# A hybrid decoder block on one Trainium2 core: scaling the last output tiles on ScalarE and POOL, and taking the root of x's normalisation in PSUM

## The chip, the core and the metric

The kernel runs on one core of one Trainium2 chip. The metric is the time of one execution in device microseconds. The kernel before was timed three times: 2665.58, 2668.71 and 2671.58 us, median 2668.71 us.

The engines are named as the profile names them: PE is TensorE (PEld its weight loads), DVE is VectorE, ACT is ScalarE, POOL is GpSimd, SP issues all the DMAs that this text speaks of. SBUF is the on-chip working memory, PSUM the eight banks into which PE writes.

## The reference, cut to what matters

One layer of a decoder block on 2048 tokens of 1024 channels. A normalised and modulated input goes through one wide projection; two branches (a causal convolution and an RWKV-7 state recurrence) work on its parts, are projected, merged and projected once more; the result is added to x and normalised by a root mean square.

```python
h = _rmsnorm(x, norm_g) * (1.0 + scale) + shift           # x's normalisation
p = h @ w_in                                              # 1024 x 9344
y_conv = _conv_branch(...); y_rwkv = _rwkv7_branch(...)   # each ends in a 1024 x 1024 product
m = sigmoid(g_conv) * y_conv + sigmoid(g_rwkv) * y_rwkv
x = x + gate * (m @ w_out)
return _rmsnorm(x, final_g)                               # y * rsqrt(mean(y*y) + eps) * final_g

def _rmsnorm(x, g):
    y = x * lax.rsqrt(jnp.mean(x * x, axis=-1, keepdims=True) + RMS_EPS)
    return y * g
```

## The kernel before, in words

**Stages.** The tokens go in four blocks of 512. For each block the wide projection runs as 73 tiles of 128 output channels, each summed over eight pieces of the 1024 input channels; each fp32 product is made as three products of halves (`h_hi,w_hi`, `h_lo,w_hi`, `h_hi,w_lo`), so 24 matmuls of 128x512 a tile, written to `ps_main`. Beside it the convolution runs on DVE (`acc<-u,ck,acc`), and the recurrence runs in groups of heads as a chain of small matmuls (`aux`, `late`, `xo`) with DVE, ACT and POOL between them. A stage of output products follows: the RWKV branch's, the convolution branch's and the last one (`ro`, `co`, `o`), for blocks 0 and 1 and then for blocks 2 and 3, each as seven products of quarter matrices whose weights are called `w_c`. The last of them, `o` on blocks 2 and 3, ends the program.

**x's normalisation** (`xnorm`, L736). It is made for block b+1 while block b is worked on: ACT squares the tiles of x and leaves row sums in the small tile `st` (the profile calls it `ss`; 128 partitions by five rows of four numbers). When all are there, DVE adds the two halves of the sums (L758), divides and adds epsilon (L759), and takes the reciprocal root by `rsteps` (L380): a first guess from the bits and three Newton rounds of three instructions, ten small instructions of 128x4, with a wait for DVE's queue before every third. All operands are in SBUF. PE then turns the four columns into rows (`late<-ident,ss`, into the only PSUM bank tagged `late`), ACT copies them, and two DMAs spread them over the partitions. That happens three times in the program, for blocks 1, 2 and 3. The bank `late` is also used by the recurrence's chains and by other norms. For the last block's convolution norm the kernel has a second form of the root, `proot` (L392), that already runs with its variance and its running product in PSUM.

**The end** (`final`, L2210, inner function `finish`, L2252 to L2280). The last product leaves 16 tiles of 128x512 (two blocks `b_`, four groups of 128 tokens `n`, two halves `h_`). For each, DVE adds x to the PSUM result, ACT squares it and leaves the row sum in `sqm` (block 3) or `sqn` (block 2). For each pair of halves DVE takes the root as eight 128x1 instructions (the profile's `v<-sqm` or `v<-sqn` and seven `v<-v`), then scales both tiles by root and `final_g` in one instruction each (`scalar_tensor_tensor`, `cells<-cells,v,fg` or `fc<-fc,v,fg`), and SP sends each tile out.

**What sets the order.** Nothing in the program runs by itself: it is written as tasks (Python generators) that yield conditions, and a model of the engines' times (`note`, L118) decides which task goes on next: `ok(t)` waits until a tile is ready by the model, `idle("DVE", ...)` until DVE's queue is nearly empty, `bank("late")` until that PSUM bank is free, `burst` adds a lag for PE. The same model picks POOL or DVE for some subtractions (`w_lo`, `w_c`, `h_lo`). So an edit to one task moves the instructions of the others, for the rest of the program.

Of the kernel before, what the change touches and what calls it, by code (L numbers as in the profile page):

```python
# [13 lines left out]
ALU = mybir.AluOpType  # L14
# [4 lines left out]
P = 128  # L19
D = 1024  # L20
KT = D // P
TB = 512
NTT = TB // P
# [36 lines left out]
AHEAD = 0.7  # L60
# [24 lines left out]
def hybrid_block(ctx: ExitStack, tc: tile.TileContext, x, x_t, vecs, convk, w2a2, final_g, ada, w_in, w_co, w_ro, w_o, crow, out,  # L85
# [127 lines left out]
    nc = Lanes()  # L213
# [41 lines left out]
    def ok(*aps):  # L255
        ks = [key(a) for a in aps]
        return lambda: max(ready[q] for q in ks)
# [5 lines left out]
    def idle(name, us):  # L263
        return lambda: vt[name] - us
# [24 lines left out]
    def burst(*ws):  # L289
        w = both(*ws)  # L290

        def f():
            r = w()
            if r is None:
                return r
            return r + lag[0]

        return f
# [437 lines left out]
    def xnorm(b, tts):  # L736
        if not tts:
            return
        if tts[0] == 0:
            sums_[b] = e2.tile([P, 5, NTT], F32, name="ss0", tag="ss0", bufs=1)  # L740
        st = sums_[b]
        for tt in tts:
            t0 = b * TB + tt * P
            xh = []
            yield hx.room(2, 1)
            for half in range(2):
                xt = hx.take("xt")
                nc.sync.dma_start(xt, x[t0:t0 + P, half * TB:half * TB + TB])
                xh.append(xt)
            for half in range(2):  # L750
                yield ok(xh[half])
                nc.scalar.activation(xh[half], xh[half], AF.Square, accum_out=st[:, half, tt:tt + 1])
                hx.give(xh[half])
        if tts[-1] + 1 < NTT:
            return
        vs, rs, t_ = st[:, 2, :], st[:, 3, :], st[:, 4, :]
        yield both(ok(st), idle("DVE", AHEAD + 0.1))
        nc.vector.tensor_tensor(out=vs, in0=st[:, 0, :], in1=st[:, 1, :], op=ALU.add)  # L758
        nc.vector.tensor_scalar(out=vs, in0=vs, scalar1=1.0 / D, scalar2=RMS_EPS, op0=ALU.mult, op1=ALU.add)  # L759
        for n, _ in enumerate(rsteps(rs, vs, t_)):  # L760
            if n % 3 == 0:
                yield idle("DVE", AHEAD + 0.1)
        yield burst(ok(st), free, bank("late"), hx.room(2, 1))
        pt = pl.tile([P, TB], F32, name="late", tag="late")
        nc.tensor.transpose(pt[0:NTT, 0:P], rs, ident)
        gt, row = hx.take("gt"), hx.take("xrow")
        nc.scalar.copy(gt[0:NTT, 0:P], pt[0:NTT, 0:P])
        yield ok(gt)
        nc.sync.dma_start(xrow_d[b].rearrange("(n p) -> n p", p=P), gt[0:NTT, 0:P])
        hx.give(gt)  # L770
        nc.sync.dma_start(row, xrow_d[b].unsqueeze(0).broadcast_to([P, TB]))
        nxt = []

        def xload(k):
            nxt.append(hx.take("xf"))
            nc.sync.dma_start(nxt[-1], x_t[k, :, b * TB:b * TB + TB])

        yield hx.room(1, 1)
        xload(0)
        for k in range(KT):  # L780
            if k + 1 < KT:
                yield hx.room(1, 1)
                xload(k + 1)
            xf = nxt.pop(0)
            yield ok(xf, row)
            nc.gpsimd.tensor_tensor(out=xf, in0=xf, in1=row, op=ALU.mult)
            yield ok(xf)
            nc.scalar.activation(xf, xf, AF.Identity, scale=g_col[:, k:k + 1], bias=shift_col[:, k:k + 1])
            yield ok(xf)
            nc.sync.dma_start(xT_dram[b][k], xf)  # L790
            hx.give(xf)
        hx.give(row)
# [975 lines left out]
    with tc.manual_schedule():  # L1768
# [441 lines left out]
        def final(b0):  # L2210
            until(lambda: "sp" in more_)
            last = b0 + 2 == NB
            order_ = [(h_, b_, n) for h_, b_ in ((0, 0), (1, 1), (0, 1), (1, 0)) for n in range(4)]
            feed = Feed(fc, [x[(b0 + b_) * TB + n * P:(b0 + b_) * TB + n * P + P, h_ * TB:h_ * TB + TB]
                             for h_, b_, n in order_])
            have = {}
            sp, fg = more_["sp"], more_["fg"]
            if last:
                sq = [[sp.tile([P, 1, 2], F32, name="sqn", tag="sqn", bufs=4) for _ in range(4)]]
                s2 = [sp.tile([P, 2, 2], F32, name="sqm", tag="sqm", bufs=2) for _ in range(2)]  # L2220
                sq.append([s2[n // 2][:, n % 2:n % 2 + 1, :] for n in range(4)])
            else:
                s8 = sp.tile([P, 2, 4, 2], F32, name="sq8", tag="sq8", bufs=1)
                sq = [[s8[:, b_, n:n + 1, :] for n in range(4)] for b_ in range(2)]

            def plus(h_, b_, n, t_, ps):
                f = order_.index((h_, b_, n))
                yield feed.has(f)
                xt = feed.got[f]
                yield ok(xt)  # L2230
                nc.vector.tensor_tensor(out=t_, in0=ps, in1=xt, op=ALU.add)
                fc.give(xt)

            class Done:

                def __call__(self, h_, b_, n, t_):
                    Task(self.square(h_, b_, n, t_, oc), 1)

                def psum(self, n, ps):
                    f = order_.index((1, 0, n))  # L2240
                    yield feed.has(f)
                    xt = feed.got[f]
                    yield from padd(xt, ps, xt)
                    Task(self.square(1, 0, n, xt, fc), 1)

                def square(self, h_, b_, n, t_, home):
                    yield ok(t_)
                    fsq = sp.tile([P, TB], F32, name="fsq", tag="fsq", bufs=1)
                    nc.scalar.activation(fsq, t_, AF.Square, accum_out=sq[b_][n][:, 0, h_:h_ + 1])
                    have[b_, n, h_] = t_, home  # L2250

            def finish(b_, ns):  # L2252
                m = len(ns)
                yield when(lambda: all((b_, n, h_) in have for n in ns for h_ in range(2)))
                v3 = sp.tile([P, 3, 4], F32, name="v3", tag="v3", bufs=2)
                vs, rs, rt = [v3[:, i_, :m] for i_ in range(3)]
                yield both(ok(sq[b_][ns[0]]), idle("DVE", AHEAD))
                s_ = s8[:, b_] if m > 1 else sq[b_][ns[0]]
                if m > 1:
                    nc.vector.tensor_tensor(out=vs, in0=s_[:, :, 0], in1=s_[:, :, 1], op=ALU.add)  # L2260
                    nc.vector.tensor_scalar(out=vs, in0=vs, scalar1=1.0 / D, scalar2=RMS_EPS, op0=ALU.mult, op1=ALU.add)
                    rsqrt(rs, vs, None, nc.vector, rt)
                    nc.vector.tensor_scalar(out=rs, in0=rs, scalar1=-256.0, scalar2=None, op0=ALU.mult)
                else:
                    nc.vector.tensor_scalar(out=vs, in0=s_[:, :, 0], scalar1=s_[:, 0, 1:2], scalar2=D * RMS_EPS, op0=ALU.add,
                                            op1=ALU.add)
                    nc.vector.tensor_scalar(out=rs.bitcast(I32), in0=vs.bitcast(I32), scalar1=-0.5, scalar2=float(0x5F3759DF),
                                            op0=ALU.mult, op1=ALU.add)
                    for z_ in (3.0, 12.0, 768.0):
                        nc.vector.tensor_scalar(out=rt, in0=rs, scalar1=rs, scalar2=vs, op0=ALU.mult, op1=ALU.mult)  # L2270
                        nc.vector.tensor_scalar(out=rs, in0=rt, scalar1=z_, scalar2=rs, op0=ALU.subtract, op1=ALU.mult)
                for i, n in enumerate(ns):
                    t0 = (b0 + b_) * TB + n * P
                    for h_ in range(2):
                        t_, home = have[b_, n, h_]
                        yield both(ok(t_, rs), idle("DVE", AHEAD))
                        nc.vector.scalar_tensor_tensor(out=t_, in0=t_, scalar=rs[:, i:i + 1],
                                                       in1=fg[:, h_ * TB:h_ * TB + TB], op0=ALU.mult, op1=ALU.mult)
                        nc.sync.dma_start(out[t0:t0 + P, h_ * TB:h_ * TB + TB], t_)
                        home.give(t_)  # L2280

            for b_ in (1, 0):
                for ns in ([[0], [1], [2], [3]] if last else [[0, 1, 2, 3]]):
                    Task(finish(b_, ns), 2)
            return sums8(held(), held(), held(), Done(), plus)
# [51 lines left out]
```

## Time and profile before

| what | us |
|---|---|
| median of three runs | 2668.71 |
| the profiled execution's own time | 2668.12 |
| its span, from the first to the last instruction | 2666.4 |
| PE busy | 2588.4 |
| DVE busy | 2145.6 |
| POOL busy | 1343.5 |
| ACT busy | 1193.7 |
| PE idle while it waited for x's root (once) | 2.9 |
| from PE's last matmul to the span's end | 16.7 |

All instructions carry one line number, L196, since a helper records them; they are told apart by the names of their tiles, written out<-in. In a timeline a row is a start, a duration, an engine and an instruction; `x7` are seven in a row that belong together, and the brackets give idle time of the engine before it with what ended that. In a table by windows a row gives the stretch, then the busy time of PE, PEld, DVE, ACT and POOL with their counts, the clock that was granted to PE (1.00 is full), and DMA.

### The profile page before, as it was taken

To read this page: it belongs to the slowest core of one execution; us is meant where nothing else is said; L and a number is where in the kernel's file an instruction comes from. 1 tells how busy PE (TensorE), PEld (TensorE's weight loads), DVE (VectorE), ACT (ScalarE), POOL (GpSimd) and SP (SyncE) were. 2 spreads that over 40 slices of the span, in tenths; PEclk is the share of its full clock that TensorE was granted. 3 is DMA by queue.
4 is the path that set the end of the run, shared out by engine and by line. 5 is a ranking of instruction groups with operands and counts; after the bars stand their busy time and mean duration, and the time that the engine had idled before them with its cause. 6 is when DMAs were issued, how large, how long until landed. Compare 5 with 4: busy or idle time off the path is not lost. (4 is left out here: it accounts for less than half of the span.)

```text
span 2666.4 us, 50801 instructions
## 1 busy us (share of the span) xinstructions
PE 2588.4 (97%) x18335; PEld 2081.0 (78%) x18335; DVE 2145.6 (80%) x3631; ACT 1193.7 (45%) x2316; POOL 1343.5 (50%) x1842
## 2 busy tenths in 40 slices
PE   8999999999999999999999999999999998899997
PEld 6777887878878877888778887788887777678886
DVE  6786879798879786987687868888988678988687
ACT  6444444443344433443444343434444454456443
POOL 3575849462648374716483756483727586000000
PEclk9999999999999999999999999999999999999998
DMA  9888787887777778858786888786766787799984
GB/s 375 285 307 305 253 270 265 269 287 242 267 246 268 241 254 279 294 183 280 256 282 217 290 276 267 235 309 217 263 201 208 228 309 251 275 336 323 330 272 155
DMA packets 390559, 711.34 MB, mean 267 GB/s; under 512 B 137482, under 2 KB 141922, under 8 KB 390307
## 3 DMA queue, kind: packets, MB, share of 16 engines
q1 hardware_dynamic: 390306, 708.09, 78.7%
q8 instruction: 145, 2.38, 0.4%
q14 instruction: 108, 0.88, 0.1%
HBM read 493.82 MB, written 213.00 MB: 265 GB/s over the span
## 5 line engine op out<-in xcount | busy, mean ns | idle before, releaser
L196 PE MATMUL ps_main<-h_hi,w_lo 128*128 128x512 f32 x2304 | 923.9, 401 | 5.2 <-POOL w_lo L196 4.7
L196 PE MATMUL ps_main<-h_hi,w_hi 128*128 128x512 f32 x2304 | 923.2, 401 | 4.9 <-DVE vv L196 2.7
L196 PE MATMUL ps_main<-h_lo,w_hi 128*128 128x512 f32 x2304 | 921.5, 400 | 0.0
L196 DVE SCALAR_TENSOR_TENSOR acc<-u,ck,acc 128x512 f32<-128x512 f32 x928 | 698.4, 753 | 26.4
L196 PEld LDWEIGHTS ps_main<-h_hi,w_lo 128*128 128x128 f32 x2304 | 434.3, 188 | 102.4 <-POOL w_lo L196 6.4
L196 PEld LDWEIGHTS ps_main<-h_hi,w_hi 128*128 128x128 f32 x2304 | 434.3, 188 | 102.4 <-issue 6.7
L196 PEld LDWEIGHTS ps_main<-h_lo,w_hi 128*128 128x128 f32 x2304 | 434.2, 188 | 91.7 <-issue 4.5
L196 PE MATMUL ps_main<-h_hi,w_c 128*128 128x512 f32 x896 | 289.2, 401 | 6.7 <-POOL w_c L196 4.5
L196 ACT ACTIVATE th<-ps_main 128x512 f32<-128x512 f32 x160 | 95.7, 598 | 289.3 <-PE ps_main L196 276.5
L196 POOL TENSOR_TENSOR itmp<-La,TT 128x126 f32<-128x126 f32 (+22 forms) x496 | 199.5, 402 | 49.8 <-issue 16.4
L196 POOL TENSOR_TENSOR TT<-TT,itmp 128x126 f32<-128x126 f32 (+22 forms) x496 | 204.3, 412 | 38.9
L196 PEld LDWEIGHTS ps_main<-h_hi,w_c 128*128 128x128 f32 x896 | 170.5, 191 | 50.4 <-POOL w_c L196 6.7
L196 POOL TENSOR_TENSOR w_lo<-w_st,w_hi 128x1024 fp32r<-128x1024 f32 x60 | 145.3, 2422 | 106.6 <-ACT w_hi L196 87.0
L196 PE MATMUL ps_main<-h_lo,w_c 128*128 128x512 f32 x448 | 180.0, 402 | 7.2 <-DVE h_lo L196 7.2
L196 ACT COPY uv<-xo 64x256 f32<-64x256 f32 (+1 forms) x192 | 81.1, 439 | 196.4 <-PE xo L196 138.0
L196 DVE SCALAR_TENSOR_TENSOR S<-xo,pe,Se 64x64 f32<-64x64 f32 x512 | 123.1, 280 | 48.3 <-PE xo L196 38.5
L196 PE MATMUL ps_main<-w_c,h_hi 128*128 128x512 f32 x448 | 140.3, 393 | 0.0
L196 ACT CAST w_c<-w_raw 128x512 fp32r<-128x512 f32 x168 | 102.2, 618 | 71.8 <-DMA w_raw<-wk_o 23.0
L196 DVE TENSOR_TENSOR As<-aux,maskA 128x512 f32<-128x512 f32 x128 | 82.4, 686 | 49.9 <-PE aux L196 49.3
L196 ACT ACTIVATE Se<-S,pe 128x128 f32<-128x128 f32 x256 | 88.6, 394 | 44.5 <-DVE S L196 43.5
L196 PEld LDWEIGHTS ps_main<-h_lo,w_c 128*128 128x128 f32 x448 | 85.7, 191 | 27.5 <-DVE h_lo L196 8.5
L196 ACT ACTIVATE t<-ps_main,mu 128x512 f32<-128x512 f32 x96 | 65.9, 687 | 86.6 <-PE ps_main L196 86.1
(305 smaller groups left out, 4507.1 us busy)
## 6 DMA issues: line engine op xcount, KB each, us to landing
w_hi<-kh_in SPq DMA_DIRECT2D x219, 512.0 KB
w_lo<-kl_in SPq DMA_DIRECT2D x219, 512.0 KB
w_st<-w_in_t SPq DMA_DIRECT2D x73, 512.0 KB
kh_in<-w_hi SPq DMA_DIRECT2D x70, 512.0 KB
kl_in<-w_lo SPq DMA_DIRECT2D x70, 512.0 KB
lny<-y_d SPq DMA_DIRECT2D x80, 256.0 KB
w_raw<-wk_o SPq DMA_DIRECT2D x56, 256.0 KB
ada_st<-ada_t SPq DMA_DIRECT2D x16, 512.0 KB
```

Of the source, the lines that this page charges most:

```text
L196: r = f(*a, **k)
```

## The change

Two edits.

1. **`xnorm`.** The sum of the two halves still goes to `st` in SBUF, but the bank `late` is taken right then, ahead of the root instead of after it. The variance `vs` and Newton's running product are columns of that bank, and the root is taken by `proot`, without waits between its instructions. Only the result `rs` is in SBUF. The transpose goes into columns of the same bank, after a wait for the result and for PE.
2. **`finish`, in the last product.** For all of block 3 and for the first two token groups of block 2, 12 of the 16 tiles, DVE's scaling is replaced by two instructions: ACT multiplies the tile by the root (`nc.scalar.mul`), POOL multiplies it by `final_g`. The last four tiles (groups 2 and 3 of block 2) stay on DVE.

```diff
-        vs, rs, t_ = st[:, 2, :], st[:, 3, :], st[:, 4, :]
+        rs, sm = st[:, 3, :], st[:, 2, :]
         yield both(ok(st), idle("DVE", AHEAD + 0.1))
-        nc.vector.tensor_tensor(out=vs, in0=st[:, 0, :], in1=st[:, 1, :], op=ALU.add)
-        nc.vector.tensor_scalar(out=vs, in0=vs, scalar1=1.0 / D, scalar2=RMS_EPS, op0=ALU.mult, op1=ALU.add)
-        for n, _ in enumerate(rsteps(rs, vs, t_)):
-            if n % 3 == 0:
-                yield idle("DVE", AHEAD + 0.1)
-        yield burst(ok(st), free, bank("late"), hx.room(2, 1))
+        nc.vector.tensor_tensor(out=sm, in0=st[:, 0, :], in1=st[:, 1, :], op=ALU.add)
+        yield both(idle("DVE", AHEAD + 0.1), bank("late"), hx.room(2, 1))
         pt = pl.tile([P, TB], F32, name="late", tag="late")
+        vs = pt[:, P:P + NTT]
+        nc.vector.tensor_scalar(out=vs, in0=sm, scalar1=1.0 / D, scalar2=RMS_EPS, op0=ALU.mult, op1=ALU.add)
+        proot(rs, vs, pt[:, 2 * P:2 * P + NTT])
+        yield burst(ok(st), free)
         nc.tensor.transpose(pt[0:NTT, 0:P], rs, ident)
...
-                        yield both(ok(t_, rs), idle("DVE", AHEAD))
-                        nc.vector.scalar_tensor_tensor(out=t_, in0=t_, scalar=rs[:, i:i + 1],
-                                                       in1=fg[:, h_ * TB:h_ * TB + TB], op0=ALU.mult, op1=ALU.mult)
+                        if last and (b_ or n < 2):
+                            yield ok(t_, rs)
+                            nc.scalar.mul(t_, t_, rs[:, i:i + 1])
+                            yield ok(t_)
+                            nc.gpsimd.tensor_tensor(out=t_, in0=t_, in1=fg[:, h_ * TB:h_ * TB + TB], op=ALU.mult)
+                        else:
+                            yield both(ok(t_, rs), idle("DVE", AHEAD))
+                            nc.vector.scalar_tensor_tensor(out=t_, in0=t_, scalar=rs[:, i:i + 1],
+                                                           in1=fg[:, h_ * TB:h_ * TB + TB], op0=ALU.mult, op1=ALU.mult)
                         nc.sync.dma_start(out[t0:t0 + P, h_ * TB:h_ * TB + TB], t_)
```

How the order moves, at three places.

**The end, on DVE.** The last rows of DVE before, from its last addition on. `fc<-ps_main,fc` is the addition of x to a tile from PSUM, the `v` rows are roots, the rows with `fg` the scalings.

```order
L196 TENSOR_TENSOR fc<-ps_main,fc 128x512
L196 SCALAR_TENSOR_TENSOR cells<-cells,v_28794,fg 128x512 x2
L196 SCALAR_TENSOR_TENSOR cells<-cells,v_28829,fg 128x512
L196 SCALAR_TENSOR_TENSOR fc<-fc,v_28829,fg 128x512
L196 TENSOR_SCALAR v_28848<-sqn 128x1
L196 TENSOR_SCALAR v_28848<-v_28848 128x1 x7
L196 TENSOR_SCALAR v_28875<-sqn 128x1
L196 TENSOR_SCALAR v_28875<-v_28875 128x1 x7
...
L196 TENSOR_SCALAR v_28882<-sqn 128x1
L196 TENSOR_SCALAR v_28882<-v_28882 128x1 x7
L196 SCALAR_TENSOR_TENSOR cells<-cells,v_28882,fg 128x512
L196 SCALAR_TENSOR_TENSOR fc<-fc,v_28882,fg 128x512
```

And now, on the same engine from the second to last addition on:

```order
L196 TENSOR_TENSOR fc<-ps_main,fc 128x512
L196 TENSOR_SCALAR v_28861<-sqn 128x1
L196 TENSOR_SCALAR v_28861<-v_28861 128x1 x7
L196 TENSOR_TENSOR fc<-ps_main,fc 128x512
L196 TENSOR_SCALAR v_28891<-sqn 128x1
L196 TENSOR_SCALAR v_28891<-v_28891 128x1 x7
L196 TENSOR_SCALAR v_28913<-sqn 128x1
L196 TENSOR_SCALAR v_28913<-v_28913 128x1 x7
L196 SCALAR_TENSOR_TENSOR cells<-cells,v_28891,fg 128x512
L196 SCALAR_TENSOR_TENSOR fc<-fc,v_28891,fg 128x512
L196 SCALAR_TENSOR_TENSOR cells<-cells,v_28913,fg 128x512
L196 SCALAR_TENSOR_TENSOR fc<-fc,v_28913,fg 128x512
```

Behind the last addition stood three roots and ten scalings (four of them are at the dots); now two roots and four scalings. The root of block 2's group 1 (`v_28861`) now stands ahead of the last addition.

**x's root in block 0, on PE.** A piece of the difference; `late<-ident,ss_822` is the transpose of the root, `aux<-KR,BK` the start of a chain.

```order
+L196 MATMUL late<-ident,ss_822 4x128
+L196 MATMUL ps_main<-h_hi,w_hi 128x512
+L196 MATMUL ps_main<-h_lo,w_hi 128x512
+L196 MATMUL ps_main<-h_hi,w_lo 128x512
+L196 MATMUL ps_main<-h_hi,w_hi 128x512
+L196 MATMUL ps_main<-h_lo,w_hi 128x512
+L196 MATMUL ps_main<-h_hi,w_lo 128x512
+L196 MATMUL ps_main<-h_hi,w_hi 128x512
 L196 MATMUL aux<-KR,BK 128x128 x8
-L196 MATMUL ps_main<-h_hi,w_lo 128x512
-L196 MATMUL ps_main<-h_hi,w_hi 128x512
-L196 MATMUL ps_main<-h_lo,w_hi 128x512
-L196 MATMUL late<-ident,ss_822 4x128
```

The transpose stands 11 main matmuls and one chain start earlier than before. On DVE the sum and the eleven instructions of variance and root now stand together ahead of `KR<-k,v,E`; before, the nine of Newton's rounds stood behind it.

**The start of the output products, on POOL.** Before, from the first to the second correction of the last group's recurrence result (`uv<-uv,gst` and `uv<-uv,grs`):

```order
L196 TENSOR_TENSOR uv<-uv,gst 128x4x256
L196 TENSOR_TENSOR h_lo<-cells,h_hi 128x512 x2
L196 TENSOR_TENSOR w_c<-w_raw,w_c 128x512 x2
L196 TENSOR_TENSOR cells<-cells 128x512 x2
L196 TENSOR_TENSOR w_c<-w_raw,w_c 128x512
L196 TENSOR_TENSOR uv<-uv,grs 128x4x256
```

And now:

```order
L196 TENSOR_TENSOR uv<-uv,gst 128x4x256
L196 TENSOR_TENSOR h_lo<-cells,h_hi 128x512
L196 TENSOR_TENSOR w_c<-w_raw,w_c 128x512
L196 TENSOR_TENSOR h_lo<-cells,h_hi 128x512
L196 TENSOR_TENSOR w_c<-w_raw,w_c 128x512
L196 TENSOR_TENSOR h_lo<-cells,h_hi 128x512
L196 TENSOR_TENSOR w_c<-w_raw,w_c 128x512
L196 TENSOR_TENSOR uv<-uv,grs 128x4x256
```

Six instructions stand between the two where seven stood. Over the whole program POOL gives ten subtractions to DVE (three `w_lo`, four `h_lo`, three `w_c`). On PE the last two chains of the recurrence have moved against the main matmuls: their first `late<-Tn,As` stood behind 6726 and 7045 of the 8928 main matmuls, and now stand behind 6875 and 7008; the output products begin at the 6913th.

## Prediction

> **What bounds the kernel now.** First the page's head: PE is busy for 97% of the span.
>
> ```profile
> span 2666.4 us, 50801 instructions
> PE 2588.4 (97%) x18335; PEld 2081.0 (78%) x18335; DVE 2145.6 (80%) x3631; ACT 1193.7 (45%) x2316; POOL 1343.5 (50%) x1842
> ```
>
> So a change off PE can win only where PE stands still: 78.0 us in all. Then the windows (columns: PE, PEld, DVE, ACT, POOL busy, PE's granted clock), which show where that is.
>
> ```profile
> 0.00:100.00 100.00, 88.83 (x419) 70.86 (x420) 70.66 (x133) 62.27 (x120) 46.09 (x42) 1.00 0.94 353
> 2400.00:2550.00 150.00, 149.58 (x645) 120.81 (x644) 110.68 (x195) 82.00 (x153) 0.00 (x0) 1.00 0.90 316
> 2550.00:2630.00 80.00, 80.00 (x348) 65.02 (x347) 57.37 (x91) 38.97 (x75) 0.00 (x0) 1.00 0.74 249
> 2649.70:2666.40 16.70, 0.00 (x0) 0.00 (x0) 12.85 (x37) 0.72 (x2) 0.00 (x0) 0.59 0.42 157
> ```
>
> The last 250 us before 2649.7 have no gap, the last 16.7 have no PE at all, and POOL does nothing in any of it. The head's 11.2 us are not touched. About 50 us of gaps are spread between. The timeline of the end shows whose time the 16.7 us are.
>
> ```profile
> 2633.84 0.68 DVE L196 TENSOR_TENSOR cells<-ps_main,cells 128x512 f32<-128x512 f32 x1
> 2644.15 0.69 DVE L196 TENSOR_TENSOR fc<-ps_main,fc 128x512 f32<-128x512 f32 x1 [0.28 <-PE ps_main L196]
> 2645.41 0.21 DVE L196 TENSOR_SCALAR v<-sqm 128x1 f32<-128x1 f32 x1
> 2645.66 1.83 DVE L196 TENSOR_SCALAR v<-v 128x1 int32<-128x1 int32 x7
> 2647.40 0.68 DVE L196 TENSOR_TENSOR fc<-ps_main,fc 128x512 f32<-128x512 f32 x1
> 2649.98 0.68 DVE L196 TENSOR_TENSOR fc<-ps_main,fc 128x512 f32<-128x512 f32 x1
> 2650.58 2.07 DVE L196 SCALAR_TENSOR_TENSOR cells<-cells,v,fg 128x512 f32<-128x512 f32 x3
> 2653.23 0.20 DVE L196 TENSOR_SCALAR v<-sqn 128x1 f32<-128x1 f32 x1
> 2655.21 0.20 DVE L196 TENSOR_SCALAR v<-sqn 128x1 f32<-128x1 f32 x1
> 2662.62 0.75 DVE L196 SCALAR_TENSOR_TENSOR fc<-fc,v,fg 128x512 f32<-128x512 f32 x1
> 2663.39 0.33 SPq L196 DMA_DIRECT2D out<-fc  x1
> ```
>
> The first root ends at 2633.84, where the next addition starts. From 2644.15 on DVE has no break over 0.6 us: additions (0.60 from start to start), roots (2.0, from 2653.23 to 2655.21), scalings (0.67). Its last one ends at 2663.37, and the last DMA lands 3.03 us later, at the end of the span.
>
> **The change, part 1: the end.** Of DVE's ten scalings behind the last addition six go away, and one root moves ahead of it. By DVE's new order: PE ends a tile every 2.77 us (an addition starts on PE's release at 2644.15, so the next at 2646.92 and 2649.69). The root of group 0 of block 2 then runs to 2646.75, the third addition from 2646.92, the root of group 1 to 2649.5, the last addition from 2649.69 (0.29 earlier than now), the two last roots to 2652.3 and 2654.3, four scalings to 2657.0 (three of 0.67 and a last one of 0.75). With 3.03 us for the DMA the end comes at 2660.05 in place of 2666.4: **6.3 us** less.
>
> That holds if ACT and POOL stay behind DVE. Their prices are those of their nearest rows:
>
> ```profile
> L196 ACT ACTIVATE sq<-k,v 128x512 f32<-128x512 f32 x32 | 22.9, 715 | 4.4 <-DVE k L196 4.4
> L196 POOL TENSOR_TENSOR lny<-lny x45: 1267/1293/1752, 766.2 to 1800.5; 128x512 f32<-128x512 f32 x45
> 2648.18 0.63 ACT L196 ACTIVATE fsq<-fc 128x512 f32<-128x512 f32 x1 [2.52 <-DVE fc L196]
> 2648.72 0.19 ACT L196 ACTIVATION_READ_ACCUMULATOR fsq<-fc 128x1 f32 x1
> ```
>
> An ACT pass with a column operand takes 0.71 us, a square with its read 0.73, a POOL product 1.29 (1.75 at most). ACT has 12 passes more. The one that could hurt is the first of group 1 of block 2: it waits for DVE's root (2649.5), and behind it in ACT's queue stands the last square, which the last root needs. It is through at 2650.2, before the last addition ends at 2650.4, so nothing waits. ACT's last pass ends at about 2652.0. POOL, idle until then, starts its first product at about 2634.6 (the first root's end and an ACT pass), gets its pairs at the pace of the roots, and ends at 2653.3, 3.7 us ahead of DVE. At 1.75 a piece it would end near 2656 and hold up DVE's last scalings by at most one product: 1.3 us, the upper bound here. SP sends the tiles in the old order; the four that stay on DVE come last, so no DMA stands behind a late POOL tile.
>
> **Part 2: x's root.** Three times DVE takes the root in SBUF. In block 0 its parts lie from 162.7 to 174.4:
>
> ```profile
> 162.60:174.40 11.80, 8.40 (x46) 6.07 (x44) 11.35 (x17) 3.08 (x4) 11.41 (x13) 1.00 0.76 281
> 163.57 1.26 DVE L196 TENSOR_SCALAR ss<-ss 128x4 f32<-128x4 f32 x2
> 169.74 2.28 DVE L196 TENSOR_TENSOR ss<-ss 128x4 f32<-128x4 f32 x1
> 172.05 1.57 DVE L196 SCALAR_TENSOR_TENSOR ss<-ss 128x4 f32<-128x4 f32 x2
> 169.49 1.16 PE L196 MATMUL aux<-KR,BK 64*128 64x128 f32 x16
> PE late L196 <- DVE ss L196: 2.9, 1, 2.9
> 171.50:174.40 2.90, 0.05 (x1) 0.00 (x0) 2.73 (x7) 0.00 (x0) 2.74 (x5) 1.00 0.15 59
> 174.40:179.00 4.60, 4.57 (x25) 3.31 (x26) 1.20 (x3) 0.26 (x1) 1.63 (x5) 0.63 0.26 45
> ```
>
> An addition of 128x4 takes 2.28 us there, with POOL busy for 11.4 of the 11.8 us; the variance and the ten instructions of the root take 6.7 in all. PE, which comes to the transpose at 171.5, stands for 2.9 us, and then runs 4.6 us at a clock of 0.63, which loses another 1.7. The kernel already holds the new form once, in the last block's norm, beside a POOL that is busy throughout:
>
> ```profile
> 2155.56 0.17 DVE L196 TENSOR_SCALAR late<-late 128x4 f32<-128x4 f32 x1 [1.05 <-PE late L196]
> 2157.56 0.16 DVE L196 SCALAR_TENSOR_TENSOR ss<-late,ss 128x4 f32<-128x4 f32 x1
> 2155.50:2157.80 2.30, 2.30 (x12) 1.87 (x12) 1.88 (x12) 0.00 (x0) 2.30 (x2) 1.00 1.02 357
> ```
>
> Eleven instructions in 2.2 us, none held up. So in block 0 the root is there at about 166. PE's transpose stands 11 main matmuls (0.23 each, a twelfth of a tile's 2.77) and a chain start (1.2) earlier, at about 167.7, and need not wait: **4.6 us** less. What the root now delays is `KR` behind it on DVE, by 1 us at most, which PE takes up at 169.5; a wait of up to 0.5 there is the bound. The bank `late` is held for the root's 2.2 us longer; no chain asks for it there. The other two roots (near 700 and 1235) have no PE wait against them in the waits; like the first they free about 4.5 us of DVE each (6.7 less 2.2), and PE's own matmuls cover that: nothing.
>
> On the clock the row is 4.6 us at 0.63 after a gap of 2.9. [...]
>
> **Part 3: the order of everything else.** Past block 0 the tasks come in another order nearly to the end, and POOL hands ten subtractions to DVE. The work is the same, so only PE's gaps can change; I count nothing, with both ends from the two largest gaps that remain:
>
> ```profile
> PE late L196 <- POOL uv L196: 6.0, 1, 6.0
> 2242.30:2250.00 7.70, 6.83 (x20) 5.38 (x21) 6.10 (x6) 3.59 (x5) 6.21 (x4) 0.51 0.67 224
> 2309.99 0.79 PE L196 MATMUL ps_main<-h_lo,w_c 128*128 128x512 f32 x1 [5.96 <-DVE h_lo L196]
> 2310.00:2318.00 8.00, 8.00 (x25) 6.39 (x26) 6.89 (x12) 4.38 (x7) 0.00 (x0) 0.71 0.45 156
> ```
>
> The first costs 6.0 and, at a clock of 0.51 for 7.7 us, another 3.8: 9.8. The second 6.0 and 2.3: 8.3. Either can go, and another can come. The remaining 35 us or so lie in pieces below 4 us; an estimate of 3 to 4 us for their sum's change is a tenth of it.
>
> **Sum.** 6.3 + 4.6 = 10.9 us less. The profiled execution took 2668.12, so 2657.2; it lies 0.6 below the median of the runs, so 2657.8 for that. I take **2657.5**.
>
> **Rivals.**
>
> *POOL holds up the end's roots (no change).* DVE's roots at the end have 128x1 operands in SBUF; before, they never ran beside POOL. Beside POOL, small SBUF instructions do get stuck:
>
> ```profile
> L196 DVE TENSOR_SCALAR ss<-ss x8: 170/171/1057, 10.1 to 1228.7; 128x4 f32<-128x4 f32 x4, 128x4 int32<-128x4 int32 x4
> L196 DVE TENSOR_SCALAR gst<-gst x16: 174/175/2059, 297.6 to 2224.2; 128x16 f32<-128x16 f32 x16
> ```
>
> Even with a single tile operand they took 1.06 and 2.06 us. From the third root on, ten POOL products (13 us) run beside five roots. Block 0's root lost 4.5 us (6.7 less 2.2) to 11.4 us of POOL work, which gives 5 us here; if every product blocks, 13. At 8 the end is 1.7 us later than now, and only part 2 is left: about 2665, within 0.2%. Against it: one element per partition is the smallest case, and no row shows it blocked. [...] Chance 0.14.
>
> *New gaps where the output products begin (slower).* The last two chains now stand back to back across that point, and POOL's correction `uv` still has six subtractions ahead of it. One more gap like the 9.8 eats the gain; from 16.2 us of new gaps on the kernel is slower by over 0.2%; two give 2668.7 - 10.9 + 19.6 = 2677. For it: the chains beside the products. Against: the last chain now ends 47 main matmuls earlier. Chance 0.08.
>
> *Those gaps go (faster still).* POOL has one instruction fewer between the corrections; with the 9.8 gone, 2648. Chance 0.08.
>
> *POOL sets the end.* It would need products over 1.6 us throughout; then 2658.5, inside the forecast's own range.
>
> **How the numbers follow.** Forecast 0.66, the rivals 0.14, 0.08 and 0.08, and 0.04 for anything else. The range 2648 to 2668 goes from the gap that disappears to the blocked roots and one new gap; the forecast's own is 2653 to 2663. A measurement of this kernel can tell about 0.2%, 5.3 us, from no change: faster means below 2663.4. Faster takes the forecast less its upper edge, and the third rival: 0.70; within 0.2% the first rival, that edge and a single new gap: 0.22; slower 0.08.
>
> **What would show it.** Right: DVE's last scaling about 7.4 us after PE's last matmul, four of them behind the last root, POOL's last product ahead of that; `v` instructions still 2.0 us a root; no wait of `late` for `ss`, and all new `late` and `ss` rows near 0.17. Wrong: `v` rows of 1 us beside POOL; POOL's products as the last step of the chain that ends last; new rows of over 4 us among PE's waits between 2100 and 2400.

## The result and the profile after

The changed kernel takes 2674.55 us (median of 21 runs, 2667.12 to 2682.17), the kernel before in the same session 2667.98 (21 runs, 2662.73 to 2676.43). The ratio is 1.0022 with a 95% interval of 1.0014 to 1.0031: **slower by 5.9 us (3.7 to 8.3)**, where 10.9 us less were forecast.

The head of the page of the changed kernel answers to the first lines of the prediction. PE is busy for 6.1 us longer with the same number of instructions; DVE is busy 38.3 us less, POOL 11.0 more.

```profile
span 2669.2 us, 50791 instructions
PE 2594.5 (97%) x18335; PEld 2087.5 (78%) x18335; DVE 2107.3 (79%) x3629; ACT 1200.8 (45%) x2328; POOL 1354.5 (51%) x1844
```

**The end** came out as written. Rows of DVE, POOL and SP in order of time (start, duration), and the window from PE's last matmul to the span's end:

```profile
2648.58 5.06 POOL L196 TENSOR_TENSOR cells<-cells,fg 128x512 f32<-128x512 f32 x4 [2.11 <-ACT cells L196]
2651.46 1.83 DVE L196 TENSOR_SCALAR v<-v 128x1 int32<-128x1 int32 x7
...
2654.13 4.05 POOL L196 TENSOR_TENSOR cells<-cells,fg 128x512 f32<-128x512 f32 x3 [0.49 <-ACT cells L196]
...
2656.96 1.83 DVE L196 TENSOR_SCALAR v<-v 128x1 int32<-128x1 int32 x7
2658.86 0.69 DVE L196 TENSOR_TENSOR fc<-ps_main,fc 128x512 f32<-128x512 f32 x1
...
2661.06 1.26 POOL L196 TENSOR_TENSOR fc<-fc,fg 128x512 f32<-128x512 f32 x1 [0.17 <-ACT fc L196]
2665.42 0.75 DVE L196 SCALAR_TENSOR_TENSOR fc<-fc,v,fg 128x512 f32<-128x512 f32 x1
2666.19 0.33 SPq L196 DMA_DIRECT2D out<-fc  x1
```

```profile
2658.82:2669.20 10.38, 0.00 (x1) 0.00 (x0) 6.81 (x21) 2.05 (x4) 3.29 (x3) 0.73 0.54 202
```

The roots run beside POOL's products at their old pace (1.83 us for seven rows), POOL ends 3.9 us ahead of DVE, and behind PE there are 10.4 us in place of 16.7.

**x's root in block 0** is there at 166.8 and PE's transpose runs at 168.6; no wait of `late` for `ss` is left. But PE now waits 3.5 us for POOL's `w_lo` at 219 (the longest such wait in the first 300 us was 1.5 before):

```profile
163.38 1.22 DVE L196 TENSOR_TENSOR ss<-ss 128x4 f32<-128x4 f32 x1
164.63 0.17 DVE L196 TENSOR_SCALAR late<-ss 128x4 f32<-128x4 f32 x1
166.63 0.16 DVE L196 SCALAR_TENSOR_TENSOR ss<-late,ss 128x4 f32<-128x4 f32 x1
...
222.92 0.70 PE L196 MATMUL ps_main<-h_hi,w_lo 128*128 128x512 f32 x1 [3.48 <-POOL w_lo L196]
```

**The start of the output products** is where the time went. I compare stretches between the same two points of PE's work, the ends of its 6650th and 7700th main matmul (main matmuls write `ps_main`; 72 of a block's 73 tiles do, one goes to `ps_f`, so the output products begin at the 6913th). The last two chains and the first products lie between them in every kernel here (1001 to 1003 other PE instructions each). Before and after:

```profile
2045.20:2364.60 319.40, 295.88 (x2055) 233.15 (x2054) 262.72 (x438) 148.89 (x283) 142.78 (x148) 0.97 0.81 269
```

```profile
2043.20:2374.20 331.00, 300.84 (x2053) 237.92 (x2052) 254.52 (x447) 147.79 (x280) 131.64 (x149) 0.95 0.79 263
```

The stretch is 11.6 us longer: 6.6 us more in which PE stands still (30.2 for 23.5), and 5.0 us in which the same matmuls take longer at a lower clock (0.95 in place of 0.97). PE's waits in it (total, times, longest), of before and of after; the 6.0 for `POOL uv`, which the prediction showed, belongs to the first list:

```profile
PE ps_main L196 <- DVE h_lo L196: 8.4, 4, 6.0
PE ps_main L196 <- POOL w_c L196: 4.5, 4, 1.7
```

```profile
PE ps_main L196 <- DVE h_lo L196: 14.0, 8, 6.0
PE late L196 <- DVE Tn L196: 4.9, 1, 4.9
PE ps_main L196 <- ACT h_hi L196: 4.0, 4, 1.5
PE xo L196 <- DVE uv L196: 2.5, 4, 1.0
...
PE late L196 <- POOL uv L196: 0.8, 1, 0.8
```

The gap for `uv` has nearly gone, which was one of the rivals; the operands `h_hi` and `h_lo` of the products and a chain's `Tn` have come in its place. The last chain now follows directly on the one before it, with no product between them:

```profile
2149.61 0.64 PE L196 MATMUL xo<-uv,As 128*64 128x64 f32 x16
2155.12 0.23 PE L196 MATMUL late<-Tn,As 32*32 32x32 f32 x1 [4.86 <-DVE Tn L196]
```

The windows behind it:

```profile
2155.10:2160.00 4.90, 3.54 (x67) 2.89 (x68) 3.81 (x8) 2.77 (x5) 4.90 (x4) 0.50 0.95 319
2160.00:2170.00 10.00, 10.00 (x204) 7.96 (x204) 4.88 (x17) 2.54 (x5) 7.07 (x6) 0.57 0.57 216
```

The clock is 0.50 and 0.57 in these 15 us, means over the two windows. The way there can be followed on SP's queue. Each chain needs eight transfers `As<-dT`, its inverted triangles. Before, those of the second to last chain go out together, 5 us behind the stores of `dT`, and the last group's `dA<-As` follow them:

```profile
2047.44 1.34 SPq L196 DMA_DIRECT2D dT<-TT  x2
2052.85 5.13 SPq L196 DMA_DIRECT2D As<-dT  x8
2062.94 7.93 SPq L196 DMA_DIRECT2D dA<-As  x8
```

After, `dA<-As` stand first, and the eight reads are spread over 21 us:

```profile
2057.41 1.59 SPq L196 DMA_DIRECT2D dT<-TT  x2
2059.06 6.56 SPq L196 DMA_DIRECT2D dA<-As  x8
2071.04 1.24 SPq L196 DMA_DIRECT2D As<-dT  x2
2079.94 2.25 SPq L196 DMA_DIRECT2D As<-dT  x4
2091.93 1.43 SPq L196 DMA_DIRECT2D As<-dT  x2
```

So that chain begins at 2100.1 in place of 2068.5. Its buffers are lent to the products when it has ended, so the products' first inputs (`cells<-z_d`) are loaded from 2150.3 on in place of 2130.7.

### The profile page after: what moved, and what is told of

It is laid out like the page before. It is cut to its first block, busy times and chain, and to the rows that moved or that the text cites. A ratio compares the mean times of both kernels' runs of the same rounds, so it can differ in the third digit from the quotient of the medians.

```text
span 2669.2 us, 50791 instructions
## 1 busy us (share of the span) xinstructions
PE 2594.5 (97%) x18335; PEld 2087.5 (78%) x18335; DVE 2107.3 (79%) x3629; ACT 1200.8 (45%) x2328; POOL 1354.5 (51%) x1844
## 5 line engine op out<-in xcount | busy, mean ns | idle before, releaser
L196 POOL TENSOR_TENSOR cells<-cells,fg 128x512 f32<-128x512 f32 x10 | 12.8, 1298 | 394.2 <-ACT cells L196 394.0
L196 PE MATMUL ps_main<-h_lo,w_c 128*128 128x512 f32 x448 | 181.9, 406 | 13.9 <-DVE h_lo L196 12.5
L196 POOL TENSOR_TENSOR w_lo<-w_st,w_hi 128x1024 fp32r<-128x1024 f32 x57 | 139.6, 2449 | 104.4 <-ACT w_hi L196 90.2
```

Source lines behind the costliest of these rows:

```text
L196: r = f(*a, **k)
```

## The experiments

**Theory A**: both edits gain what was forecast, and the new order that edit 1 gives to the rest of the program loses more. **Rivals**: B, the new end costs in timed runs; C, the root's place in PSUM (the bank held longer) costs. Times below are differences to the runs of the kernel before on the same chip, worked out as (ratio - 1) x 2668 us, with the interval.

### Place and order apart

Edit 2 alone, and edit 1 alone, are the two halves of the diff above. For the third kernel the operands of x's root are in PSUM, but the planner's model is told the old instructions, and the task waits as it did, so that every engine keeps before's order:

```diff
+        pt = pl.tile([P, TB], F32, name="late", tag="late")
+        pv, pq, dve = pt[:, P:P + NTT], pt[:, 2 * P:2 * P + NTT], tc.nc.vector
...
-        for n, _ in enumerate(rsteps(rs, vs, t_)):
-            if n % 3 == 0:
-                yield idle("DVE", AHEAD + 0.1)
...
+        for _ in range(3):
+            yield idle("DVE", AHEAD + 0.1)
+            dve.scalar_tensor_tensor(out=pq, in0=rs, scalar=-0.5, in1=pv, op0=ALU.mult, op1=ALU.mult)
+            note("DVE", "tensor_tensor", t_, [rs, rs], 0.0, [rs, rs])
...
```

`dve` issues an instruction without telling the model, and `note` tells it the old one.

The fourth is its mirror: edit 1's order, with `sm` and `t_` of `st` as the real operands and the model told of PSUM.

> Edit 2 alone: the end's scalings on ScalarE and POOL, everything ahead of them instruction for instruction as before. Theory A (the loss comes from the new order that edit 1 gives to the whole program, the end is a gain as forecast): 6.3 us under before, 2661.7 us beside 2668.0, ratio 0.9976; PE's last matmul ends where it does before (2649.7), 10.4 us ahead of the last store's issue's neighbourhood as in the changed kernel instead of 16.8. Rival B (the end itself costs when it is timed, and what the trace of the changed kernel shows there is only its one execution): no gain or a loss, 2668 to 2671.

Measured: 2660.76 us, ratio 0.9974 (0.9965 to 0.9983), 6.9 us less. Rival B falls.

> Edit 1 alone: the root of x's normalisation in PSUM with the new waits of its task, the end as before. Theory A: the changed kernel's PE end (9.2 us later than before) with before's tail, so 6.3 us over the changed kernel: 2680.9 us, ratio 1.0047 to before. Rival B (the end costs, the root gains): 2666 or less. Rival C (the root's place, its 11 instructions and the bank that it holds, costs): the same 2680.9 as theory A, told apart by the next two.

Measured: 2680.79, ratio 1.0050 (1.0033 to 1.0067), 13.3 us more.

> Both edits, but the planner is told the old instructions and the old waits for x's root, so that every engine's order is before's own, with only the operands in PSUM. Theory A: block 0's stall goes (4.3 us by the aligned traces) and the end gives 6.3: 2657.4 us, ratio 0.9960, PE's last matmul near 2645.4. Rival C (the place costs): not under the kernel with edit 2 alone, 2662 to 2671, with PE's end as late as the changed kernel's at the worst.

Measured: 2657.23, ratio 0.9963 (0.9948 to 0.9978), 9.9 us less: both edits without their order. This beats both kernels.

> The order that edit 1 gives, instruction for instruction, but variance and running product of the root stay in SBUF; the end as before. Theory A: the loss stays, and the 3 to 4 us that PSUM saves in block 0 are lost on top: 2681 to 2685 us, ratio 1.005 to 1.0065. Rival C (the place costs): back to before's 2668, ratio 1.000. In both the bank is held from the same place on, so a cost of holding the bank alone would show here as in edit 1 alone and not in the kernel with before's order.

Measured: 2684.45, ratio 1.0065 (1.0049 to 1.0081), 17.3 us more. Rival C falls as well: the order costs 17.3 with the root in SBUF, and moving it to PSUM takes 3.7 off that (2684.45 to 2680.79) in the new order and 3.5 (2660.76 to 2657.23) in the old one. The intervals of each pair overlap, but the traces have the same size: over all kernels PE's 600th main matmul ends at 206.3 on average with the root in PSUM and at 209.9 without. The stretch at the start of the products took 319.4 us in the first, 320.5 in the third, 331.6 and 328.9 in the second and fourth: it goes with the order, not with the place. The first of these, where the row of before had 319.40 too:

```profile
2048.20:2367.60 319.40, 295.47 (x2054) 232.41 (x2053) 263.08 (x438) 148.93 (x283) 142.94 (x148) 0.97 0.80 270
```

### Which block's root moves the order

The first branch holds edit 1's root, the second the old one; the complement has `b in (3,)`.

```diff
+        if b in (1, 2):
...
+        else:
...
```

> The new root of edit 1 for x's second and third blocks (used in the kernel's blocks 0 and 1), the old one for the fourth; the end as before. The order differs from before's up to PE's row 3285 of 11443 and is before's own from there on. Theory A2 (the loss is made only where the order of the output products' beginning changes, which the fourth block's root sets off): the early part keeps what the aligned traces of the changed kernel show at 456 us, 2.4 us, or up to 4: 2664 to 2667 us, ratio 0.9985 to 0.9995, and no loss between 2100 and 2290 us. Rival (any new order costs, spread over the program): over before, 2670 or more.

Measured: 2667.56, ratio 1.0000 (0.9988 to 1.0012). Nothing: less than was expected of it, and the interval is 3.2 us to either side. What takes back the 3.5 us of the root is not shown: its trace has a wait of 2.7 us like the one for `w_lo` above, but PE's 4000th main matmul still ends 3.4 us ahead of before's, and the last one 2.6 us ahead. The stretch took 318.7 us.

> The complement: the new root for x's fourth block alone (used in the kernel's block 2). The order is before's up to PE's row 5617, and behind row 5830 nearly that of the changed kernel: the last two recurrence chains begin behind main products 6875 and 7008 as there (6726 and 7045 before). Theory A2: all the loss and none of the gain: 10 to 13 us over before, 2679 to 2682 us, ratio 1.0038 to 1.005, with 10 to 12 us of it between 2100 and 2290 us. Rival (spread): about half of edit 1 alone's loss, 2674.

Measured: 2680.48, ratio 1.0047 (1.0029 to 1.0065), 12.5 us more, and a stretch of 330.0 us. As theory A2 has it: the fourth block's root, against which the trace of before shows no PE wait, makes nearly all of edit 1's net loss of 13.3 us.

### What in the new order it is

Two causes were at hand in the trace of the changed kernel: H1, late inputs of the products; H2, the two chains back to back. The first kernel is before with late lending, the second edit 1 alone with the last chain held back.

```diff
             yield when(lambda: Gs[-2].chained)
+            yield after(20.0)
             l3_cells(sc, "As", "As", "tk", "tk", "KR", "KR")
```

```diff
         yield when(lambda: G.pairs == 2 and (before is None or before.chained))
+        if (b, g) == (NB - 1, 3):
+            yield after(15.0)
```

> Before, but the second to last chain's As, tk and KR buffers are lent to the output products 20 us later by the planner's clock than that chain's end; nothing ahead of PE's row 9944 changes, and the last chain moves up to main product 6957. Rival H1 (late loads of the products' inputs are what costs): the changed kernel's loss without its other changes, 6 to 11 us over before, 2674 to 2679. H2 (the last chain directly behind the second to last, with no product between, is what costs): the second to last chain stays at 6726, so at most 3 us, 2666 to 2671.

Measured: 2672.44, ratio 1.0018 (1.0005 to 1.0030), 4.8 us more (1.3 to 8.0). This lies between the two, and the interval meets both the 6 to 11 of H1 and the 3 at most of H2: late inputs are a part of the loss at best.

> Edit 1 alone with the last chain held back 15 us by the planner's clock, so that it begins behind main product 7053 (7008 there, 7045 before); nothing ahead of PE's row 9983 changes, the cells are lent as late as there. H1: no recovery, 2678 to 2684 us as edit 1 alone (2680.8). H2: the wait of 4.9 us for Tn, the 1.3 behind it and the lower clock from 2140 to 2180 us (7 us) go in good part, 5 to 10 us under edit 1 alone: 2671 to 2676.

Measured: 2680.81, ratio 1.0045 (1.0029 to 1.0061), no recovery. H2 falls as a cause of its own: the wait for `Tn` went, and others stood in its place.

```profile
PE ps_main L196 <- ACT h_hi L196: 7.8, 2, 4.3
PE late L196 <- POOL uv L196: 6.8, 1, 6.8
```

Next the swap on SP's queue by itself: before with the reads behind, edit 1 alone and the changed kernel with the reads first, and as a control the rule that puts them first in the kernel before, where they are first anyway. The first piece puts the reads behind, the second and third put them first.

```diff
         yield ok(dT)
+        if (b, g) == (NB - 1, 2):
+            yield when(lambda: Gs[-1] is not G and Gs[-1].stored)
...
+        if (b, g) == (NB - 1, 3):
+            yield when(lambda: before.read)
         dA = dp.tile([2, 2, NCH // 2, 2, 2, 32, 32], F32, name="dA", tag="dA", bufs=2)
...
-                yield idle("SP", 0.1)
+                if (b, g) != (NB - 1, 2):
+                    yield idle("SP", 0.1)
+        G.read = True
```

> Before, with one thing changed: the eight transfers As<-dT that bring the second to last recurrence chain its inverted triangles are issued behind the last group's transfers dA<-As and La<-dA on SP's queue, not ahead of them, as it came out in the changed kernel. Nothing ahead of it differs (PE's order is before's up to row 9560 of 11443); the last two chains then begin behind main products 6874 and 7008 (6726 and 7045 before; 6875 and 7008 in the changed kernel). Theory A3 (this place on SP's queue is the source of the loss at the start of the output products): 9 to 12 us over before, 2677 to 2680 us, ratio 1.0034 to 1.0045, all of it between 2045 and 2370 us. Rival (the loss needs the other reorderings ahead of it as well): 0 to 5 us, 2668 to 2673.

Measured: 2680.55, ratio 1.0048 (1.0029 to 1.0067), 12.8 us more. This one swap is enough for a loss of the whole size, with no other change ahead of it. SP's queue, then the stretch, then two of PE's longest waits in it:

```profile
2052.43 8.41 SPq L196 DMA_DIRECT2D dA<-As  x8
2063.47 1.07 SPq L196 DMA_DIRECT2D As<-dT  x2
...
2087.48 0.98 SPq L196 DMA_DIRECT2D As<-dT  x2
```

```profile
2039.10:2370.70 331.60, 301.80 (x2054) 238.55 (x2053) 256.97 (x443) 149.05 (x283) 130.70 (x141) 0.94 0.77 259
```

```profile
PE late L196 <- DVE Tn L196: 4.8, 1, 4.8
PE ps_main L196 <- ACT h_hi L196: 3.8, 3, 1.9
```

> Edit 1 alone, with the reverse: the last group's dA<-As wait until the chain before has issued its eight As<-dT, one behind the other; the order ahead of SP's row 1449 is that of edit 1 alone. The last two chains begin behind 6777 and 7060. Theory A3: most of the loss goes, 7 to 11 us under edit 1 alone (2680.8): 2670 to 2674 us, ratio 1.001 to 1.0025. Rival: 2677 or more.

Measured: 2681.31, ratio 1.0046 (1.0032 to 1.0060). A miss: nothing comes back, though the second to last chain begins behind main product 6777 in place of 6875. PE waits 7.9 us for `w_c` from POOL instead (0.2 in the changed kernel, 4.5 before):

```profile
PE ps_main L196 <- POOL w_c L196: 7.9, 3, 4.6
PE ps_main L196 <- DVE h_lo L196: 7.4, 2, 6.6
PE late L196 <- POOL uv L196: 5.3, 1, 5.3
```

> The changed kernel (both edits) with the same rule. Theory A3: 6.3 to 8.2 us less than the run before it: 2663 to 2667 us, ratio 0.998 to 0.9997. Rival: as the changed kernel or worse, 2672 or more.

Measured: 2672.44, ratio 1.0010 (1.0000 to 1.0020). By the ratios it is 2.7 us over before, 3.2 us under the changed kernel's 5.9, with intervals that overlap: a miss too.

> A control: the same rule in the kernel before, where the eight transfers are issued together anyway and the last group's follow them. The last two chains begin behind 6731 and 7059 (6726 and 7045). Theory A3: within 2 us of before, 2666 to 2670 us, ratio 0.9992 to 1.0008. Rival (any touch of this order moves the time by 5 us or more): outside of that.

Measured: 2676.71, ratio 1.0033 (1.0018 to 1.0048), 8.8 us more. The control failed, and theory A3 with it: the swap is sufficient, but it is not what the loss hangs on. A touch that was meant to do nothing cost nearly as much.

### Is it the touch itself

Two theories were left. P: the loss grows with what is pushed back. D: before's order at this place is a favourable one, and nearly any other is worse. Four nudges in the kernel before, of 1 and 3 us of the planner's clock, at the two places where the kernels with late lending and with the held chain have 20 and 15:

```diff
+            yield after(1.0)
```

> Before, with the second to last chain's buffers lent to the output products 1 us later by the planner's clock. PE's order is before's up to row 9964, and only 122 lines of it differ behind that; the last chain begins behind main product 7057 (7045). Theory P (the loss has a price that grows with what is pushed back: late inputs, chains back to back): within 2 us of before, ratio 0.9993 to 1.0007. Theory D (before's order here is a drawn and kept one, and nearly any other is worse by several us, whatever its reason): 4 to 10 us over before, 1.0015 to 1.004.

Measured: 2668.84, ratio 1.0004 (0.9992 to 1.0015).

> The same with 3 us (last chain behind 7055, 274 lines of PE's order differ). Theory P: within 2 us, at most 3. Theory D: 4 to 10 us over before.

Measured: 2680.03, ratio 1.0043 (1.0029 to 1.0057), 11.5 us more.

> Before, with the last chain held 1 us by the planner's clock: behind main product 7047 in place of 7045, PE's order before's up to row 10007. Theory P: within 2 us. Theory D: 4 to 10 us over before.

Measured: 2675.76, ratio 1.0033 (1.0021 to 1.0045), 8.8 us more.

> The same with 3 us: behind main product 7055. Theory P: within 2 us. Theory D: 4 to 10 us over before. Over the four, theory D allows one that is as good as before, not four.

Measured: 2675.58, ratio 1.0030 (1.0018 to 1.0041), 8.0 us more.

Theory P falls: three of the four are outside its 2 us, and 3 us of later lending cost 11.5 where 20 us cost 4.8. Theory D gave what was seen, three kernels 8.0 to 11.5 us slower (4 to 10 were expected) and one as good as before, but it names no reason. For the lending 3 us later, the stretch and three of PE's waits in it:

```profile
2044.60:2377.30 332.70, 302.91 (x2054) 239.07 (x2053) 261.92 (x442) 151.18 (x284) 141.81 (x147) 0.94 0.78 263
```

```profile
PE late L196 <- POOL uv L196: 6.4, 1, 6.4
PE ps_main L196 <- ACT w_c L196: 5.6, 2, 4.1
PE ps_main L196 <- POOL w_c L196: 4.3, 2, 3.4
```

No wait for `Tn` here, and `uv` and POOL's `w_c` cost about what they did before (6.0 and 4.5). ACT's `w_c` is new (5.6 for 1.3), and of the 13.3 us 7.0 are PE busy for longer, at a granted clock of 0.94 in place of 0.97. All kernels together (the stretch is from one profiled execution each, the time from the timed runs):

| order of the stretch | stretch, us | time against before, us |
|---|---|---|
| before's own: before, edit 2 alone, both edits, blocks 1 and 2 | 319.4, 319.4, 320.5, 318.7 | 0, -6.9, -9.9, 0.0 |
| edit 1's: changed, edit 1 alone, in SBUF, block 3 | 331.0, 331.6, 328.9, 330.0 | 5.9, 13.3, 17.3, 12.5 |
| reads behind | 331.7 | 12.8 |
| reads first: in edit 1, in the changed kernel, in before | 326.1, 330.3, 329.6 | 12.3, 2.7, 8.8 |
| lending 1, 3 and 20 us later | 323.4, 332.7, 325.4 | 1.1, 11.5, 4.8 |
| last chain held by 1 and 3 us; by 15 in edit 1's | 324.8, 327.2; 326.7 | 8.8, 8.0; 12.0 |

Four kernels with before's order lie within 1.8 us of one another. Every other order of the stretch is 4 to 13 us longer in its one trace. Differences of 4 us say little there: the reads-first rule gives edit 1 alone and the changed kernel the same order in this stretch, and the two took 326.1 and 330.3. So lending 1 us later (323.4) cannot be told from before, as its time has it too (1.1, -2.1 to 4.0); all others are at least 5 us longer.

What stays open: why before's order is the best of these. The waits that replace its own are different ones each time (`Tn`, `h_hi`, `h_lo`, `w_c`, `uv`), and no single one was found whose removal brings the time back. That SP's queue came out swapped in the changed kernel because POOL had finished the triangle's inversion 10 us later (`dT<-TT` at 2057.41 for 2047.44) is read from the trace and was not tried by itself.

## Why the prediction was wrong, point by point

1. **The end, 6.3 us less: right.** 6.9 alone (4.5 to 9.3), 6.4 in the traces' tails. POOL's first product, the pace of the roots and the four scalings behind the last one are as worked out.
2. **The rival of roots held up by POOL: wrong**, as its low chance had it. The seven `v<-v` from 2651.46 on lie wholly beside POOL's four products of 2648.58 to 2653.64, those from 2656.96 on begin beside three that fill 2654.13 to 2658.18, and both take 1.83 us, as the seven from 2645.66 on before, with POOL idle. The rows that spoke for the rival, of 128x4 and 128x16, had taken up to 1.06 and 2.06 us; why those of 128x1 do not is not shown.
3. **x's root in block 0, 4.6 us less: right in its mechanism, over-sized.** The wait is gone, and the place in PSUM is worth 3.5 to 3.7 us by the times. PE's 600th main matmul ends at 205.8 to 206.5 with the root in PSUM and at 208.7 to 211.7 without it, in all kernels run.
4. **The other two roots, counted at nothing: false for what it left out.** As instructions they have no PE wait against them in the trace of before (`late` waits for `ss` once, 2.9 us, in block 0). But the root of the fourth block is the edit that rearranges the start of the output products, and with it alone the kernel is 12.5 us slower.
5. **Part 3, the order of everything else, "I count nothing": the step that failed.** The new order costs 17.3 us (13.1 to 21.6), measured with the root in SBUF. By stretches of PE's work, as means over the profiled executions of seven kernels with edit 1's order and eleven with before's in that stretch: 1.8 between main matmuls 600 and 4000, 4.7 from there to 6650, 10.8 from 6650 to 7700 (four and four). The sum of the three is 17.3; single executions scatter by 2 to 3 us, so the first is not clear of zero. Less the 6.9 of the end and the 3.7 of the root that makes 6.7 us more; measured were 5.9. "Only PE's gaps can change" was too narrow as well: 5.0 of the 11.6 us are the same matmuls at a lower clock (0.95 in place of 0.97), which the prediction had priced only behind the gaps that it listed.
6. **The bounds of that step were drawn from gaps that exist.** The 9.8 us of `uv` did shrink, as one rival had it, and the 8.3 of `h_lo` stayed. What came is new, and no gap of before had to be there for it. "The remaining 35 us or so" were taken to vary by a tenth, 3 to 4 us; the stretch alone, its large gaps included, came out 5 to 13 us longer in every other order but one, and shorter in none.
7. **The rival that came had a chance of 0.08:** new gaps where the output products begin, deciding from 16.2 us on. Its place was right for 10.8 of the 17.3 us; the rest lies ahead of it. What spoke against it, that the last chain ends 47 main matmuls earlier, was no protection: the second to last had moved 149 later. Nor is their standing back to back the cause by itself: the kernel before with the two brought together loses 12.8 us (reads behind), but edit 1 with the two apart still loses 12.0 and 12.3 (chain held, reads first). Which wait decides stays open.

The chances failed with the same step: a term with no sign was taken to be centred on zero. Here no other order of the stretch was faster than before's, so the changes went one way. That before's had been kept as the best of many would explain it, but no run shows that.

## What to carry to other kernels

An edit that passes through a planner is two changes: the instructions, and the order of everything behind them. Price the second from what small nudges cost at the places where PE depends on several engines in turn; in this kernel five of seven touches of one stretch of before cost 8 to 13 us, about as much as the two edits gain. Where the planner's model can be told the old instructions, the edit can be had without its order: here that makes 9.9 us less out of 5.9 us more.

## What the runs showed of the hardware

PE's clock fell in the changed kernel's stretch without a long gap. It was 0.96 from 2250 to 2258, in which PE had no break. In the next 8 us PE stood still for 4.6, in pieces of at most 1.7; then it ran at 0.68:

```profile
2258.00:2266.00 8.00, 3.43 (x11) 1.58 (x9) 7.22 (x12) 4.90 (x8) 0.00 (x0) 0.89 1.05 405
2266.00:2274.00 8.00, 7.85 (x24) 6.25 (x25) 5.94 (x11) 4.85 (x11) 0.00 (x0) 0.68 1.02 388
```

By an estimate from the second row its 7.85 us of PE's work hold 2.5 us of loss (7.85 x 0.32). What made the clock fall is not shown: no run changed these waits alone.

The same order did not take the same time in each execution. Four executions of before's order agreed within 1.8 us in the stretch, but two of another order differed by 4.2 (326.1 and 330.3), and PE's last matmul ended 3.0 us apart (2649.64 and 2652.61) in the kernel before and the one with edit 2 alone, whose PE order is the same.
